# Inverted blocks loaded in 8 transfers instead of 16, diagonal blocks stored in 4 instead of 16, in a bidirectional gated-delta encoder layer

## The chip, the cores and the metric

The kernel runs on one core of a Trainium2 chip. The metric is the device time of one launch in microseconds (us). A core has five engines that run in parallel and wait for each other by semaphores: PE (TensorE, matrix products into PSUM), DVE (VectorE), ACT (ScalarE), POOL (GpSimd) and SP (SyncE), which here issues nearly all DMA transfers. Each engine works through its own instructions strictly in order, so an instruction that waits holds up everything behind it on that engine.

## The reference

One encoder layer over two sequences, a prompt of 1024 tokens and a sample of 256. A combined input projection feeds two groups of heads: four heads of a bidirectional gated DeltaNet and four heads of differential attention; then come an output projection, a layer norm, a SwiGLU and a second layer norm. The change lies in the delta rule, which is computed in chunks, forwards and backwards:

```python
def delta_rule_chunked(q, k, v, g, beta):
    ...
    gc = jnp.cumsum(g, axis=-1)
    decay = jnp.exp(jnp.where(incl, gc[..., :, None] - gc[..., None, :], -jnp.inf))
    kb = k * beta[..., None]
    m = jnp.where(strict, jnp.einsum('bhnid,bhnjd->bhnij', kb, k) * decay, 0.0)
    a_mat = m + jnp.eye(CHUNK, dtype=jnp.float32)
    rhs = jnp.concatenate([v * beta[..., None], kb * jnp.exp(gc)[..., None]], -1)
    sol = lax.linalg.triangular_solve(a_mat, rhs, left_side=True, lower=True, unit_diagonal=True)
    ...
    attn = jnp.einsum('bhnid,bhnjd->bhnij', q, k) * decay
    ...
    _, o = lax.scan(step, s0, xs)

    o_f = delta_rule_chunked(q, k, v, g[:, :, 0], beta[:, :, 0])
    o_b = flip(delta_rule_chunked(flip(q), flip(k), flip(v), flip(g[:, :, 1]), flip(beta[:, :, 1])))
```

The kernel uses chunks of 128 and inverts each chunk's unit triangular matrix explicitly.

## The kernel before

Four phases follow each other. Phase A (0 to about 523 us on PE) computes the input projection in columns of 128 (`dense_T`, matmuls of line 172) and, between these, prepares the DeltaNet. Phase B runs attention (score products of lines 835 and 836) together with the recurrent chains (`chain`, from line 1006 on). Phases C and D are the output projection, layer norms and the SwiGLU.

The preparation works in five *units*: units 1 to 4 are the heads of the prompt (8 chunks each), unit 5 is the sample (4 heads of 2 chunks). A unit passes through these steps:

- `prep_front` and, for two groups of four chunks, `prep_group`. Products of keys with keys and queries (`kq_ps`, line 418) are scaled by ACT into the tile KQ (line 424), the backward query products are copied there (line 426), and DVE multiplies by the decays `e_f`, `e_b`, `e_n` (lines 435 and 441). The results N[0] (forward) and N[1] (backward) are the matrices to be inverted; their diagonal blocks of 32 x 32 go to DRAM scratch `nblk` (line 438).
- `invert_blocks`: the blocks of the whole unit come back as 128 rows of 1024 in the tile Wb (line 465), each block in one partition, and DVE inverts them in Ub by products and sums (lines 470 and 471; tmp is the tile itmp). It begins with line 474.
- `spread_blocks`: Ub goes to DRAM scratch `ublk` with t = 0 (line 508), its transpose with t = 1, through Wb (lines 509 and 510), and from there onto the diagonals of four tiles UD (line 514).
- `invert_levels`: PE, ACT and DVE build the full inverses from the diagonal blocks, in four stages (`inv_ps`, line 535). The first stage multiplies N by the t = 1 tiles. The result goes to the records `rec` (line 578), from which phase B loads the chains' operands (`ld`, line 969).

UD, Wb, Ub and itmp exist once, so that a unit can fill them only when the unit before has been read out. The tiles of phase B lie in memory that phase A has used, so the first `ld` waits for the end of unit 5's inverse.

The order of the instructions on each engine is not written out in the source. The units are Python generators that `advance()` steps once per half of a dense product, levels first, then blocks, then fronts:

```python
        def advance():
            stage_of(levels, None)
            stage_of(blocks_, levels)
            stage_of(fronts, blocks_, HP_F)
            run_all(gens)
```

From what the source emits, the tile framework's scheduler then chooses each engine's order when the program is built, by priority and by when it reckons the operands to be ready. A small edit can thus move instructions far away from it.

Of the kernel before, what the change touches and what calls it, by code (L numbers as in the profile page):

```python
# [334 lines left out]
def prep_front(k, si, vh, c3, G, N, flag, room):  # L335
# [6 lines left out]
    for g in range(2):  # L342
# [12 lines left out]
        sq = gp.tile([P, 16, P], F32, tag="kq", name="sq")[:, 0:8]  # L355
# [15 lines left out]
    N.extend(k.gp2.tile([P, 8, P], F32, tag=f"N{d}", name=f"N{d}") for d in range(2))  # L371
    for g in range(2):
        yield from prep_group(k, si, vh, g, raw, G, N)


def prep_group(k, si, vh, g, raw, G, N):
# [36 lines left out]
    KQ = gp.tile([P, 4, 4, P], F32, tag="kq", name="KQ")  # L413
    for j in range(2):
# [11 lines left out]
        A.copy(KQ[:, 2 * j:2 * j + 2, 3], ps.rearrange("p (a b c) -> p a b c", a=2, b=2)[:, :, 1])  # L426
# [7 lines left out]
    def to_blocks(d, e):  # L434
        V.tensor_tensor(out=N[d][:, u0:u0 + 4, :], in0=KQ[:, :, 2 * d, :], in1=e, op=ALU.mult)
        for b in range(4):
            r = slice(32 * b, 32 * b + 32)
            nc.sync.dma_start(out=k.S.nblk[si][vh][d, u0:u0 + 4, b].rearrange("u r c -> r u c"), in_=N[d][r, u0:u0 + 4, r])

    def attn(d, e):  # L440
        V.tensor_tensor(out=e, in0=KQ[:, :, 1 + 2 * d, :], in1=e, op=ALU.mult)
# [16 lines left out]
def invert_blocks(k, si, vh):  # L458
# [42 lines left out]
    return Wb  # L501


def spread_blocks(k, si, vh, Wb):
# [4 lines left out]
    V.tensor_copy(Wb[0:64].rearrange("p (a b) -> p a b", a=32), U[0:64].rearrange("p (b a) -> p a b", a=32))  # L509
    nc.sync.dma_start(out=k.S.ublk[si][vh][1].rearrange("d u b r c -> (d u b) (r c)"), in_=Wb[0:64])  # L510
    for t in (1, 0):
        for b in range(4):
            for d in range(2):
                nc.sync.dma_start(out=diag(k, d, t, b), in_=k.S.ublk[si][vh][t][d, :, b].rearrange("u r c -> r u c"))


def diag(k, d, t, b):

# [4 lines left out]
def invert_levels(k, si, vh, N, G):
# [37 lines left out]
    for d in range(2):  # L561
        U, D = k.UD[d]
# [1097 lines left out]
```

## Time and profile before

| | before |
|---|---|
| time, median of 3 runs | 1794.15 us (1793.14 to 1796.1) |
| profiled execution: time, span | 1791.56 us, 1789.8 us |
| mean granted clock of PE | 0.970 |
| PE busy | 1710.3 us, 96% |
| DVE, ACT, POOL busy | 68%, 44%, 12% |
| PE idle, waiting for loads of UD | 12.1 us in 8 waits |
| PE idle, waiting for the first `ld` | 8.9 us in one wait |
| SP: loads of UD, stores to nblk | 80 and 80 |

Rows of instructions give start (us from the span's start), duration (us), engine, source line, operation, output tile <- input tiles, shape and count, and in brackets the idle time of the engine before them and what ended it. "SPq" is the issue of a DMA on SP: its duration is the time on the queue, not that of the transfer. In a table of windows each engine's busy time is followed by its number of instructions in brackets; the clock is the share of full speed that PE was granted.

### The profile page before, as it was taken

The page shows a single profiled execution, that of the slowest core. Times are in us where ns is not written, and L with a number is a line of the kernel's source. Part 1 is how long each engine was busy: PE and PEld are TensorE (multiplying, and loading weights), DVE is VectorE, ACT ScalarE, POOL GpSimd, SP SyncE. Part 2 cuts the span into 40 slices and gives each one's busy share as a digit, 9 for nine tenths or more (in the row PEclk, how much of TensorE's full clock was granted, in tenths as well). Part 3 has the DMA queues.
Part 4 walks back from the last instruction along what each step waited for, and adds up shares of the span by engine and source line. Part 5 has one row for each costly group of instructions (what it writes and reads, how often), then busy time and mean ns, then how long its engine had stood idle before and what let it go on. Part 6 is the DMA issues. An engine that isn't in the chain of part 4 may idle for free.

```text
span 1789.8 us, 27447 instructions
## 1 busy us (share of the span) xinstructions
PE 1710.3 (96%) x10234; PEld 1483.0 (83%) x10234; DVE 1214.0 (68%) x2092; ACT 783.7 (44%) x1538; POOL 218.5 (12%) x201
## 2 busy tenths in 40 slices
PE   8999989999986899999999999999999999999998
PEld 8988868888864898788888888888888887888886
DVE  4245888986694468977665866665666665666696
ACT  4146766664433767877113332322222223553330
POOL 2000000000022435732321000000000000000011
PEclk9999999998985999999999999999999999999999
DMA  7124456656754977634631534333344432975541
GB/s 237 40 57 115 126 131 168 168 168 182 190 154 103 297 238 220 177 118 156 188 119 51 193 112 140 120 121 133 124 145 146 146 113 100 386 272 177 174 159 71
DMA packets 254116, 279.05 MB, mean 156 GB/s; under 512 B 49297, under 2 KB 198687, under 8 KB 252575
## 3 DMA queue, kind: packets, MB, share of 16 engines
q1 hardware_dynamic: 244079, 265.20, 47.6%
q10 hardware_dynamic: 9904, 12.10, 2.0%
q8 instruction: 80, 1.31, 0.3%
q14 instruction: 53, 0.43, 0.1%
HBM read 183.80 MB, written 93.43 MB: 155 GB/s over the span
## 4 chain that ended last, share of the span: by engine, by line
PE 54%; ACT 1%; DVE 1%; issue 1%; DMA 0%; POOLq 0%; POOL 0%; DVEq 0%; SPq 0%; ACTq 0%
PE dn_ps L1503 14%; PE gy_ps L1277 9%; PE gs_ps L1277 7%; PE om_ps L172 6%; PE gx_ps L1277 6%; PE gz_ps L1277 6%; PE gp_ps L1277 2%; PE o_ps L875 1%; PE x_ps L1182 0%; ACT ap L839 0%; PE s_ps L835 0%; PE tt_ps L862 0%; PE s_ps L836 0%; DVE ast L837 0%; ACT woh L1162 0%
## 5 line engine op out<-in xcount | busy, mean ns | idle before, releaser
L1293 ACT CAST sph<-wraw 128x512 fp32r<-128x512 f32 x92 | 57.0, 623 | 195.7 <-PE gy_ps L1277 124.5
L310 POOL TENSOR_TENSOR rs_r<-lva,mhalf 128x1 f32<-128x1 f32 x20 | 29.5, 1475 | 837.4 <-DVE lva L1139 818.9
L172 PE MATMUL dps<-xh,wlo 128*128 128x512 f32 (+1 forms) x552 | 122.7, 363 | 2.0 <-DVE wlo L163 2.0
L172 PE MATMUL dps<-xl,whi 128*128 128x512 f32 (+1 forms) x552 | 122.4, 364 | 0.0
L172 PE MATMUL dps<-xh,whi 128*128 128x512 f32 (+1 forms) x552 | 122.2, 362 | 0.0
L1293 ACT CAST sph<-wsum 128x512 fp32r<-128x512 f32 x80 | 49.7, 622 | 156.6 <-PE gy_ps L1277 61.9
L1503 PE MATMUL dn_ps<-tth,ssh 128*128 128x512 f32 x280 | 108.9, 389 | 0.0
L1503 PE MATMUL dn_ps<-ttl,ssh 128*128 128x512 f32 x280 | 108.8, 389 | 0.0
L172 PEld LDWEIGHTS dps<-xh,wlo 128*128 128x128 f32 x552 | 94.4, 193 | 17.3 <-DVE wlo L163 2.4
L1503 PE MATMUL dn_ps<-tth,ssl 128*128 128x512 f32 x280 | 108.1, 389 | 0.0
L172 PEld LDWEIGHTS dps<-xl,whi 128*128 128x128 f32 x552 | 94.8, 195 | 15.8 <-ACT whi L162 0.4
L172 PEld LDWEIGHTS dps<-xh,whi 128*128 128x128 f32 x552 | 94.1, 193 | 14.4
L329 DVE SCALAR_TENSOR_TENSOR c<-pad,cw,c 128x1024 f32<-128x1024 f32 (+1 forms) x96 | 81.7, 876 | 28.8 <-ACT c L327 28.3
L837 DVE TENSOR_REDUCE ast<-s_ps 128x1 f32<-128x1024 f32 (+1 forms) x80 | 83.5, 1055 | 22.6 <-PE s_ps L836 20.4
L1294 DVE TENSOR_TENSOR spl<-wraw,sph 128x512 fp32r<-128x512 f32 x92 | 63.0, 686 | 47.9 <-PE gs_ps L1277 29.6
L839 ACT ACTIVATE ap<-s_ps,ast 128x1024 f32<-128x1024 f32 (+1 forms) x80 | 79.8, 1000 | 34.7 <-DVE ast L837 32.1
L1294 DVE TENSOR_TENSOR spl<-wsum,sph 128x512 fp32r<-128x512 f32 x80 | 55.0, 688 | 46.8 <-issue 20.4
L835 PE MATMUL s_ps<-akl,aq 128*128 128x512 f32 (+1 forms) x144 | 65.8, 458 | 20.3 <-ACT ap L839 19.0
L1494 ACT CAST ssh<-sraw 128x640 fp32r<-128x640 f32 x77 | 55.9, 727 | 48.5 <-PE dn_ps L1503 34.3
L1495 DVE TENSOR_TENSOR ssl<-sraw,ssh 128x640 fp32r<-128x640 f32 x77 | 62.9, 820 | 16.8 <-ACT ssh L1494 13.4
L851 POOL TENSOR_TENSOR ap<-ap,ap 128x512 f32<-128x512 f32 (+2 forms) x60 | 62.4, 1059 | 81.2 <-ACT ap L848 49.5
L875 PE MATMUL o_ps<-av,tt 128*128 128x128 f32 x544 | 66.2, 280 | 0.0
(391 smaller groups left out, 4307.6 us busy)
## 6 DMA issues: line engine op xcount, KB each, us to landing
ld<-rec SPq DMA_DIRECT2D x160, 192.0 KB, 3.9
sraw<-hs SPq DMA_DIRECT2D x77, 320.0 KB, 4.7
wraw<-in_w_gate_up_dram SPq DMA_DIRECT2D x22, 1024.0 KB, 5.2
wraw<-in_w_in_dram SPq DMA_DIRECT2D x24, 512.0 KB, 4.2
wdraw<-in_w_down_dram SPq DMA_DIRECT2D x11, 1024.0 KB, 4.9
ws<-wdraw SPq DMA_DIRECT2D x11, 1024.0 KB, 3.9
traw<-ws SPq DMA_DIRECT2D x44, 256.0 KB, 4.1
araw<-dqk SPq DMA_DIRECT2D x40, 256.0 KB, 5.0
```

What stands on the lines that cost most here:

```text
L172: nc.tensor.matmul(out, lhsT=a(i), rhs=b(i), start=start and j == 0, stop=stop and j == len(seq) - 1)
L329: V.scalar_tensor_tensor(out=out, in0=pad[:, so + w:so + w + n], scalar=k.cw[:, w * 12 + ti:w * 12 + ti + 1], in1=out, op0=ALU.mult, op1=A ...
L835: nc.tensor.matmul(ps[:, o:o + w], lhsT=a.q[m][:, qs], rhs=a.kl[m][:, k0 + o:k0 + o + w], start=True, stop=False)
L837: V.tensor_reduce(out=st[:, m:m + 1], in_=ps, op=ALU.max, axis=AX.X, negate=True)
L839: A.activation(p, ps, AF.Exp, bias=st[:, m:m + 1], accum_out=a.s0[:, i:i + 1] if m == 0 else st[:, 2:3])
L851: nc.gpsimd.tensor_tensor(out=pr[0][:, c], in0=pr[0][:, c], in1=pr[1][:, c], op=ALU.add)
L875: nc.tensor.matmul(ps[:, j * P:(j + 1) * P], lhsT=tt[:, i, j * P:(j + 1) * P], rhs=a.v[:, v0 + i, :], start=i == 0, stop=i == NT[a.si] - 1)
L1277: m = nc.tensor.matmul(ps, lhsT=a(i), rhs=b(i), start=start and j == 0, stop=stop and j == len(seq) - 1, skip_group_check=again)
L1293: A.copy(hi, src)
L1294: V.tensor_tensor(out=lo, in0=src, in1=f32(hi), op=ALU.subtract)
L1495: V.tensor_tensor(out=lo, in0=src, in1=f32(hi), op=ALU.subtract)
L1503: nc.tensor.matmul(ps, lhsT=a[:, c], rhs=b, start=z == 0 and j == 0, stop=z == NPR - 1 and j == 2)
```

## The change

The four UD tiles (two of them half as wide) become two of 128 x 16 x 128, one for t = 0 and one for t = 1, with the forward and the backward direction beside each other, and N[0] and N[1] become halves of one tile of the same shape. One transfer now moves a block row of both directions: 8 loads of twice the size for 16 of `ublk`, and 4 stores for 16 of `nblk`, which are issued once both groups are ready. The transposed blocks leave through itmp instead of Wb. The backward query products are no longer copied into KQ: DVE multiplies them by `e_b` from PSUM, half a group at a time, and `e_b` is therefore computed before the products.

```diff
@@ prep_front
-    N.extend(k.gp2.tile([P, 8, P], F32, tag=f"N{d}", name=f"N{d}") for d in range(2))
+    both = k.gp2.tile([P, 16, P], F32, tag="N", name="N")
+    N.extend(both[:, 8 * d:8 * d + 8] for d in range(2))
     for g in range(2):
         yield from prep_group(k, si, vh, g, raw, G, N)
+    for b in range(4):
+        r = slice(32 * b, 32 * b + 32)
+        nc.sync.dma_start(out=k.S.nblk[si][vh][:, :, b].rearrange("d u r c -> r (d u) c"), in_=both[r, :, r])
@@ prep_group
-    KQ = gp.tile([P, 4, 4, P], F32, tag="kq", name="KQ")
+    e_b = gp.tile([P, 4, P], F32, tag="e_b", name="e_b")
+    masked(e_b, e_n, k.lower, ALU.add)
+    decay(e_b, 1, 1.0)
+    KQ = gp.tile([P, 4, 3, P], F32, tag="kq", name="KQ")
...
-        A.copy(KQ[:, 2 * j:2 * j + 2, 3], ps.rearrange("p (a b c) -> p a b c", a=2, b=2)[:, :, 1])
+        V.tensor_tensor(out=e_b[:, 2 * j:2 * j + 2], in0=ps.rearrange("p (a b c) -> p a b c", a=2, b=2)[:, :, 1],
+                        in1=e_b[:, 2 * j:2 * j + 2], op=ALU.mult)
+    nc.sync.dma_start(out=rec[:, :, 7, :], in_=e_b)
...
     def to_blocks(d, e):
         V.tensor_tensor(out=N[d][:, u0:u0 + 4, :], in0=KQ[:, :, 2 * d, :], in1=e, op=ALU.mult)
-        for b in range(4):
-            r = slice(32 * b, 32 * b + 32)
-            nc.sync.dma_start(out=k.S.nblk[si][vh][d, u0:u0 + 4, b].rearrange("u r c -> r u c"), in_=N[d][r, u0:u0 + 4, r])
-
-    def attn(d, e):
-        V.tensor_tensor(out=e, in0=KQ[:, :, 1 + 2 * d, :], in1=e, op=ALU.mult)
-        nc.sync.dma_start(out=rec[:, :, 1 + 6 * d, :], in_=e)
@@ spread_blocks
-    V.tensor_copy(Wb[0:64].rearrange("p (a b) -> p a b", a=32), U[0:64].rearrange("p (b a) -> p a b", a=32))
-    nc.sync.dma_start(out=k.S.ublk[si][vh][1].rearrange("d u b r c -> (d u b) (r c)"), in_=Wb[0:64])
+    V.tensor_copy(k.itmp[0:64].rearrange("p (a b) -> p a b", a=32), U[0:64].rearrange("p (b a) -> p a b", a=32))
+    nc.sync.dma_start(out=k.S.ublk[si][vh][1].rearrange("d u b r c -> (d u b) (r c)"), in_=k.itmp[0:64])
     for t in (1, 0):
         for b in range(4):
-            for d in range(2):
-                nc.sync.dma_start(out=diag(k, d, t, b), in_=k.S.ublk[si][vh][t][d, :, b].rearrange("u r c -> r u c"))
+            nc.sync.dma_start(out=diag(k, t, b), in_=k.S.ublk[si][vh][t][:, :, b].rearrange("d u r c -> r (d u) c"))
@@ phase_a
-        k.UD = [[per.tile([P, 8, P if d == t else 64], F32, name=f"UD{d}{t}") for t in range(2)] for d in range(2)]
+        k.UD = [per.tile([P, 16, P], F32, name=f"UD{t}") for t in range(2)]
```

`invert_levels` has the same products as before, with other slices of the tiles. In the rows below, the numbers behind tile names only tell tiles apart; before, UD_1060 to UD_1063 are the four tiles (1061 and 1063 are t = 1), in the changed kernel UD_1060 is t = 0 and UD_1061 is t = 1.

SP, between the inversions of units 3 and 4. Before, the end of unit 3's sixteen loads of UD, then the last store of unit 4's blocks (nblk_68) and the load of its Wb:

```order
L514 DMA UD_1060<-ublk_70 32x8x32
L514 DMA UD_1062<-ublk_70 32x8x32
L514 DMA UD_1060<-ublk_70 32x8x32
L514 DMA UD_1062<-ublk_70 32x8x32
L514 DMA UD_1060<-ublk_70 32x8x32
L514 DMA UD_1062<-ublk_70 32x8x32
L438 DMA nblk_68<-N_3452 32x4x32
L354 DMA rec_65<-vn 512x1x128
L465 DMA Wb<-nblk_68 64x1024 x2
```

The same place in the changed kernel:

```order
L377 DMA nblk_68<-N 32x16x32 x4
L182 DMA wraw<-in_w_in_dram 128x8x128
L445 DMA rec_66<-e_f 512x1x128
L464 DMA Wb<-nblk_68 64x1024
L506 DMA ublk_70<-Ub 64x1024
L464 DMA Wb<-nblk_68 64x1024
L508 DMA ublk_70<-itmp 64x1024
L399 DMA e_f<-gc_57 128x512
L354 DMA rec_65<-vn 512x1x128
L511 DMA UD_1060<-ublk_70 32x16x32 x4
L511 DMA UD_1061<-ublk_70 32x16x32 x4
```

The loads of unit 4's Wb moved from behind unit 3's spread to before it, behind a load of weights (wraw), and the t = 1 tile is now loaded after the t = 0 tile.

PE, after the last dense product. Before, fourteen pairs of score products (s_ps) stand ahead of unit 5's first inverse products (inv_ps from N); the last of them and these:

```order
L835 MATMUL s_ps<-akl,aq 128x512
L836 MATMUL s_ps<-akh,aq 128x512
L535 MATMUL inv_ps<-UD_1061,N_4209 32x32 x8
L535 MATMUL inv_ps<-UD_1063,N_4210 32x32 x8
L835 MATMUL s_ps<-akl,aq 128x512
L836 MATMUL s_ps<-akh,aq 128x512
L835 MATMUL s_ps<-akl,aq 128x512
L836 MATMUL s_ps<-akh,aq 128x512
L535 MATMUL inv_ps<-UD_1061,N_4209 32x32 x8
L535 MATMUL inv_ps<-UD_1063,N_4210 32x32 x8
```

In the changed kernel, from the last dense product on:

```order
L172 MATMUL dps<-xh_291,whl 128x256 x16
L828 MATMUL s_ps<-akl,aq 128x512
L829 MATMUL s_ps<-akh,aq 128x512
L828 MATMUL s_ps<-akl,aq 128x512
L829 MATMUL s_ps<-akh,aq 128x512
L828 MATMUL s_ps<-akl,aq 128x512
L530 MATMUL inv_ps<-UD_1061,N 32x32 x32
L829 MATMUL s_ps<-akh,aq 128x512
L828 MATMUL s_ps<-akl,aq 128x512
L829 MATMUL s_ps<-akh,aq 128x512
```

The first inverse products of unit 5 moved from behind 28 score matmuls to behind five. Four score matmuls make a group (one map of one tile of queries).

DVE, the end of unit 5's inversion. Before, up to the transpose into Wb, with score maxima (ast) and a query part (aq) between its products:

```order
L470 TENSOR_TENSOR itmp<-Ub,iT 128x1024
L837 TENSOR_REDUCE ast<-s_ps 128x1
L471 TENSOR_REDUCE Ub<-itmp 128x8x8
L837 TENSOR_REDUCE ast<-s_ps 128x1
L470 TENSOR_TENSOR itmp<-Ub,iT 128x1024
L837 TENSOR_REDUCE ast<-s_ps 128x1
L802 SCALAR_TENSOR_TENSOR aq<-araw,aq 64x1024
L471 TENSOR_REDUCE Ub<-itmp 128x8x8
L841 RECIPROCAL ast<-ast 128x1
L837 TENSOR_REDUCE ast<-s_ps 128x1
L507 COPY Ub<-Ub 64x16x8
```

In the changed kernel:

```order
L469 TENSOR_TENSOR itmp<-Ub,iT 128x1024
L470 TENSOR_REDUCE Ub<-itmp 128x8x8
L795 SCALAR_TENSOR_TENSOR aq<-araw,aq 64x1024
L469 TENSOR_TENSOR itmp<-Ub,iT 128x1024
L470 TENSOR_REDUCE Ub<-itmp 128x8x8
L505 COPY Ub<-Ub 64x16x8
L507 COPY itmp<-Ub 64x1024
L830 TENSOR_REDUCE ast<-s_ps 128x1
L539 COPY Z<-inv_ps 32x16x32 x2
```

All four score maxima moved behind the inversion.

More of the change, by code (lines that the diff above doesn't have):

```diff
@@ L354, in prep_front @@
                 nc.sync.dma_start(out=k.S.rec[si][vh][g][:, :, 5, :], in_=vn)
-        sq = gp.tile([P, 16, P], F32, tag="kq", name="sq")[:, 0:8]
+        sq = gp.tile([P, 12, P], F32, tag="kq", name="sq")[:, 0:8]
         for role in range(2):
@@ L435, in to_blocks @@
         V.tensor_tensor(out=N[d][:, u0:u0 + 4, :], in0=KQ[:, :, 2 * d, :], in1=e, op=ALU.mult)
-        for b in range(4):
-            r = slice(32 * b, 32 * b + 32)
-            nc.sync.dma_start(out=k.S.nblk[si][vh][d, u0:u0 + 4, b].rearrange("u r c -> r u c"), in_=N[d][r, u0:u0 + 4, r])
-    def attn(d, e):
-        V.tensor_tensor(out=e, in0=KQ[:, :, 1 + 2 * d, :], in1=e, op=ALU.mult)
-        nc.sync.dma_start(out=rec[:, :, 1 + 6 * d, :], in_=e)
     to_blocks(0, e_f)
-    attn(0, e_f)
+    V.tensor_tensor(out=e_f, in0=KQ[:, :, 1, :], in1=e_f, op=ALU.mult)
+    nc.sync.dma_start(out=rec[:, :, 1, :], in_=e_f)
     yield
-    attn(1, e_b)
     to_blocks(1, e_n)
@@ L500, in invert_blocks, with spread_blocks @@
         prod(8, 8, 16, (U, a * 32, [[32, 8], [0, 8], [1, 16]]), (T, 0, [[0, 8], [1, 8], [8, 16]]), (U, 16 + a * 32, [[32, 8], [1, 8]]))
-    return Wb
-def spread_blocks(k, si, vh, Wb):
+def spread_blocks(k, si, vh):
     nc, V, U = k.nc, k.nc.vector, k.Ub
@@ L526, in invert_levels @@
     q = [slice(32 * b, 32 * b + 32) for b in range(4)]
-    hq = [slice(32 * (b % 2), 32 * (b % 2) + 32) for b in range(4)]
-    uq, dq = (q, hq), (hq, q)
     lo, up = slice(0, 64), slice(64, 128)
-    ub = (up, lo)
+    UD = [[t[:, 8 * d:8 * d + 8] for t in k.UD] for d in range(2)]
     def pe(ps, rows, c0, m, fn):
@@ L619, in phase_a @@
             nc.gpsimd.memset(pad, 0.0)
-        k.UD = [[per.tile([P, 8, P if d == t else 64], F32, name=f"UD{d}{t}") for t in range(2)] for d in range(2)]
-        for row in k.UD:
-            for t in row:
-                nc.gpsimd.memset(t, 0.0)
+        k.UD = [per.tile([P, 16, P], F32, name=f"UD{t}") for t in range(2)]
+        for t in k.UD:
+            nc.gpsimd.memset(t, 0.0)
         k.upper, k.lower = [per.tile([P, P], F32, name=n) for n in ("m_up", "m_low")]
@@ L668, in invert @@
             def invert():
-                flag.Wb = yield from invert_blocks(k, si, vh)
+                yield from invert_blocks(k, si, vh)
             def back():
-                spread_blocks(k, si, vh, flag.Wb)
+                spread_blocks(k, si, vh)
                 yield from invert_levels(k, si, vh, N, k.G[si])
```

32 lines of the change are left out of this document (14 added, 18 removed).

## The prediction

> **What bounds the kernel now.** I read the page's shares first, then what TensorE (PE) waits for, and then the stretch in which those waits lie. The page's first part, and its rows of PE's busy tenths and of the granted clock in 40 slices of 44.7 us:
>
> ```profile
> PE 1710.3 (96%) x10234; PEld 1483.0 (83%) x10234; DVE 1214.0 (68%) x2092; ACT 783.7 (44%) x1538; POOL 218.5 (12%) x201
> ...
> PE   8999989999986899999999999999999999999998
> ...
> PEclk9999999998985999999999999999999999999999
> ```
>
> PE is busy for 96% of the span, and the change adds and removes no matmul. What it can move is PE's idle time and the time at a low clock, and both gather in the slices from about 525 to 590 us. Two of the three longest waits of PE (in total, times, longest one, us):
>
> ```profile
> PE inv_ps L535 <- DMA UD<-ublk: 12.1, 8, 5.0
> PE vn_ps L1023 <- DMA ld<-rec: 8.9, 1, 8.9
> ```
>
> Both belong to the code that is changed: the blocks of the inverse that are loaded into UD, and the records from which the recurrent chains start. PE in order of time, from the first score group (s_ps), which follows the last dense product, to the first chain product (vn_ps):
>
> ```profile
> 523.15 0.40 PE L835 MATMUL s_ps<-akl,aq 128*128 128x512 f32 x1
> ...
> 547.60 1.93 PE L535 MATMUL inv_ps<-UD,N 32*32 32x32 f32 x32 [1.10 <-DMA UD<-ublk]
> 549.46 0.80 PE L835 MATMUL s_ps<-akl,aq 128*128 128x512 f32 x1
> ...
> 551.46 1.91 PE L535 MATMUL inv_ps<-UD,N 32*32 32x32 f32 x32
> ...
> 583.57 0.77 PE L1023 MATMUL vn_ps<-ld,ld 128*128 128x128 f32 x2 [8.94 <-DMA ld<-rec]
> ```
>
> The dense products end at 523.2 us. The inverse of the last unit (unit 5, the sample) gets its operands only at 547.6, and the chains, which need the memory that the inverse frees, start at 583.57. This tail of 60 us holds eleven score groups and one inverse, about 18 us of work at full clock (eleven groups of 1.0, half of the 2.0 from 549.46 to 551.46 at half clock; 224 matmuls of the inverse, of which the two rows above show 64 in 3.84 at half clock). I take it as what the change acts on. Windows around it (duration, busy PE, PEld, DVE, ACT, POOL, then clock, DMA share, GB/s):
>
> ```profile
> 400.00:425.00 25.00, 22.73 (x235) 19.62 (x234) 10.38 (x18) 7.74 (x16) 2.89 (x1) 0.82 0.67 167
> 425.00:472.00 47.00, 47.00 (x287) 40.15 (x286) 44.96 (x76) 33.23 (x80) 0.00 (x0) 0.99 0.70 202
> 472.00:492.00 20.00, 18.65 (x220) 15.44 (x219) 4.53 (x9) 1.57 (x4) 0.00 (x0) 1.00 0.67 169
> 492.00:541.00 49.00, 37.59 (x213) 30.66 (x212) 46.09 (x71) 18.49 (x28) 9.64 (x3) 0.80 0.59 153
> ...
> 550.00:560.00 10.00, 10.00 (x114) 7.90 (x113) 6.69 (x8) 3.08 (x4) 2.27 (x2) 0.50 0.15 24
> ```
>
> Here VectorE (DVE) sets the pace: it is full in 425-472 and 492-541, where it inverts the diagonal blocks of units 4 and 5, and it stands idle for 14.6 and 15.5 us in the two stretches between. Why it stands idle is in the rows of DVE and of SP, the queue that issues the loads:
>
> ```profile
> 403.60 1.35 SPq L438 DMA_DIRECT2D nblk<-N  x1
> 405.06 9.86 SPq L514 DMA_DIRECT2D UD<-ublk  x16
> 414.96 0.45 SPq L438 DMA_DIRECT2D nblk<-N  x1
> ...
> 417.32 1.14 SPq L465 DMA_DIRECT2D Wb<-nblk  x2
> ...
> 421.99 0.18 DVE L474 COPY Ub<-Wb 128x16 f32<-128x16 f32 x1 [4.49 <-issue]
> ...
> 464.89 0.67 DVE L435 TENSOR_TENSOR N<-KQ,e_n 128x512 f32<-128x512 f32 x1
> ...
> 475.80 10.22 SPq L514 DMA_DIRECT2D UD<-ublk  x16
> 486.07 1.14 SPq L465 DMA_DIRECT2D Wb<-nblk  x2
> 492.17 0.18 DVE L474 COPY Ub<-Wb 128x16 f32<-128x16 f32 x1 [7.86 <-issue]
> ...
> 539.93 1.03 DVE L509 COPY Wb<-Ub 64x1024 f32<-64x1024 f32 x1
> ...
> 544.85 8.94 SPq L514 DMA_DIRECT2D UD<-ublk  x16
> ```
>
> A unit's inversion begins with L474 and ends with L509. Each load of Wb stands on SP behind sixteen UD loads of the unit before (9.86 and 10.22 us), because Wb also carries the transposed blocks out (L510) until their store has landed. So unit 4 begins at 421.99 though all of its stores but one had left SP by 405, and unit 5 at 492.17 though its last N was ready at 465.6.
>
> **The change part by part.**
>
> *The DMAs.* Durations on SP (first number after the count: shortest, median, longest issue in ns), and the window 544-556 us, in which the sixteen UD loads run nearly alone:
>
> ```profile
> L514 SPq DMA_DIRECT2D UD<-ublk x80: 303/449/1673, 261.5 to 553.3; - x80
> L578 SPq DMA_DIRECT2D rec<-UD x20: 512/634/802, 309.8 to 578.5; - x20
> ...
> q1 hardware_dynamic: 4442, 0.78, 32.7%
> ...
> UD<-ublk SPq DMA_DIRECT2D x16, 32.0 KB, 1.9
> ```
>
> Sixteen loads take 8.94 to 10.22 us on SP, 0.56 to 0.64 each in a run, while the DMA engines are 33% busy: the issue sets the pace. A load of twice the packets is not in the trace; its bounds are 0.56 (an issue costs the same) and 1.12 (it costs by packets). The nearest row is L578, 512 packets at 0.63; I take that, so eight loads take 5.0. The sixteen stores become four at the same price, 2.5 us where they took about 7, but none leaves before both groups are done.
>
> The Trainium skill (DMA: Bandwidth & Descriptors, section Bandwidth) calls transfers under 64 KB descriptor-dominated, and the descriptors do not become fewer here. By it eight loads would take the 8.9 us of sixteen, and the sum below would be 2 us smaller. With the engines 33% busy, this trace does not agree.
>
> *Wb no longer carries the blocks out* (itmp does), so its load needs only the four stores. On SP the loads of unit 4 move ahead of unit 3's spread. Its N were stored around 400 to 404; four stores (2.5), 2.5 to land, two Wb issues (1.14) and 4.4 to land give a start at about 412 instead of 421.99. That fills 10 of the 14.6 idle us, so that DVE has unit 4 and the N of unit 5 done at 463 rather than 472.8. From there on SP: the eight UD loads of unit 4 wait until unit 3's UD has been stored (463 + 1.3 + 3.4), their last four take 2.5 more, the stores 2.5 + 2.5, Wb 1.1 + 4.4: unit 5 starts at 480 or 481, 12 earlier, and DVE stands idle for some 10 us before it instead of 15.5.
>
> *What lies within unit 5's inversion.* Before, four score maxima and three aq were queued between its products. Over 150-580 us by form, and over 400-542 us:
>
> ```profile
> L837 DVE TENSOR_REDUCE ast<-s_ps 128x1 f32<-128x1024 f32 x11 | 13.3, 1218 | 5.2 <-PE s_ps L836 5.0
> ...
> L802 DVE SCALAR_TENSOR_TENSOR aq<-araw,aq 64x1024 fp32r<-64x1024 f32 x3 | 5.4, 1807 | 1.3 <-ACT aq L801 1.3
> ...
> L763 DVE TENSOR_TENSOR rx<-rx,rcs 128x256 f32<-128x256 f32 x5 | 2.1, 418 | 0.1
> ```
>
> Now no maximum and two aq are: 4 x 1.22 + 1.8 = 6.7 us less, and six more rope products, 2.5 more. 48.8 us (492.17 to 540.96) become 44.6 by this, so it would end at 525. By DVE's work instead (106 us of work in 400-541, less 6.7, with some 20 idle) it ends at 519. I take 522, 19 earlier.
>
> *From there to the first matmul.* The first UD load follows 3.9 us later (540.96 to 544.85), now at 526. PE's first operand was the third load and arrived 2.75 later; now it is the fourth of eight (three t = 0 loads go ahead): 3 x 0.63 + 1.9 = 3.8 plus its own issue, at 530. The halved number thus gains nothing here, its order takes it back. The dense products and the five score matmuls that stand ahead end at 524.4, so data decide: 530 instead of 547.6, **17.6 earlier**.
>
> *From the first matmul to vn_ps.* Before: 36.0 us with four score groups in it. Now 7.75 groups stand there. One takes 2.0 at the clock of this stretch: 7.5 more, from 0 to 7.5 of it hidden under the 8.94 of waiting for records and the waits for Z. I take the middle: **3.7 later**. Two groups come after vn_ps instead of before it, where the clock is full, at 1.0 each: **2.0 later**. From there the order on PE is that of before, group by group, so a shift here is a shift of the end.
>
> *Small operations*, ahead of the tail:
>
> ```profile
> L426 ACT COPY KQ<-kq_ps x20: 372/410/452, 163.3 to 450.6; 128x256 f32<-128x256 f32 x20
> ...
> L441 DVE TENSOR_TENSOR e_b<-KQ,e_b x10: 671/683/693, 167.1 to 461.6; 128x512 f32<-128x512 f32 x10
> ...
> L559 DVE COPY UD<-inv_ps x15: 417/418/432, 284.2 to 565.6; 32x256 f32<-32x256 f32 x15
> ```
>
> ScalarE (ACT) loses 20 copies, 8.2 us, at 44% busy: nothing. DVE reads PSUM in two halves, at 0.42 each by L559 (L763 gives the same from SBUF): 20 x 0.42 - 10 x 0.68 = 1.6 us more over ten groups, some 0.6 of it after 400, within the rounding above. The PSUM tile kq_ps is now held until DVE, not ACT, has read it. The next group's matmuls come about 12 us later; the cover is that distance, and if DVE falls behind by more, PE stands at kq_ps.
>
> *The dense stretch.* PE waited 12.1 us for UD there and in the tail. The first blocks of units 2 and 4 now stand 60 and 81 matmuls earlier, those of units 1 and 3 about where they stood. A gain of all of it or a like loss are the bounds; I take zero, since a later dense end is hidden until it passes 530.
>
> **Sum:** -17.6 + 3.7 + 2.0 = -11.9, and two stores that now follow the first eight record loads instead of standing among them give 1.3: **-13 us**. The profiled execution took 1791.56 (span 1789.8), 2.6 under the median of 1794.15; on the median this is **1781**.
>
> **The rivals.**
> *1. The clock stays up.* In 550-560 PE was busy for 10.0 of 10 us and the clock stood at 0.50, so the trace says that this work does not bring it back; but with PE going from dense products to inverse with a wait of 6 us instead of idling on and off from 525, it may not drop. PE's work from first matmul to vn_ps is then some 14 us instead of 29: the 3.7 vanish and half of the inverse's 13 us too: 1771. The Trainium skill (TensorE: Matmul & The Clock Gate, Part 1: The HAM clock gate) has the full clock return after one busy window of about 3.4 us, which would make this the likely case; the row of 550-560 contradicts it.
>
> *2. Unit 5 does not start earlier.* Both loads of Wb now stand behind a weight load (wraw), which waits for DVE:
>
> ```profile
> SPq L182 <- DVE wlo L163: 53.1, 11, 14.6
> ```
>
> If such a wait (longest 14.6) eats the 12 us, only the 6.7 of deferred work is left, less the 4.4 of the later terms: 1792, no change to measure or a little faster.
>
> *3. Slower: PE stands before UD in the dense stretch.* Unit 1 shows the price in the trace:
>
> ```profile
> 268.69 1.91 PE L535 MATMUL inv_ps<-UD,N 32*32 32x32 f32 x32 [5.01 <-DMA UD<-ublk]
> ...
> 272.00:276.00 4.00, 4.00 (x26) 3.29 (x25) 3.93 (x6) 1.06 (x1) 0.11 (x1) 0.51 0.90 197
> 276.00:280.00 4.00, 4.00 (x22) 3.40 (x21) 3.41 (x12) 3.02 (x6) 0.00 (x0) 1.00 0.92 270
> ```
>
> A wait of 5.0 is followed by some 7.3 us at half clock, 3.7 lost: 8.7 in all. For unit 4 the earlier place and the wait for unit 3's store leave 6 or 7 us open, 10 with the clock. It decides when the dense end passes 542: then the first matmul is not 4.4 earlier than before, which is what the later terms cost. With units 2, 3 and 4 each losing 10, the dense end is 553, the first matmul 554, and the time 1794 + 6.5 + 4.4 = 1805. Against it: so far PE's place and the data met within 2.3 us for units 2 to 4.
>
> **How the numbers follow.** The sum's case (start of the chains 6 to 20 us earlier, 1774 to 1788) gets 0.60, the clock 0.13, rival 2 0.13 (of which 0.08 within 0.2%), rival 3 0.14 (of which 0.01 within). Faster by over 0.2% (3.6 us, about what can be told from no change): 0.60 + 0.13 + 0.05 = 0.78; same 0.09; slower 0.13. The range reaches from rival 1 to a little beyond rival 2, 1766 to 1797, and leaves most of rival 3 out.
>
> **What would show it.** Right: L464 (Wb) of units 4 and 5 at about 406 and 475 on SP, the first inv_ps of unit 5 at 526 to 534, vn_ps near 570, UD loads of 0.6 us each, DVE less idle in 400-425. Wrong: UD loads of 1.1 us; a wait for UD of over 5 us in the dense stretch; dense products that end after 535; a wait at kq_ps; or a gain that lies after the chains have started.

## The result, and the profile after

| | before | after |
|---|---|---|
| median of the runs on one chip | 1793.64 us | 1768.35 us |
| ratio, 95% interval | | 0.9864 (0.9842 to 0.9886) |
| profiled execution: time, span | 1791.56, 1789.8 us | 1766.4, 1764.5 us |
| mean granted clock of PE | 0.970 | 0.975 |

The change makes the kernel 1.4% faster. The forecast was 1781, 13 us below the 1794.15 of before; the medians differ by 25.3 us, and so do the two profiled spans. The direction and the place were right, the size was half. One run of a kernel of the next section (e9, 2834 us at a clock of 0.56) is left out of its ratio.

From the first page of the changed kernel's profile come the busy times of the engines, PE's busy tenths and its granted clock, in slices of 44.1 us; from its view of waits, three of PE's (in total, times, longest one), and below them one of before:

```profile
PE 1707.8 (97%) x10234; PEld 1480.5 (84%) x10234; DVE 1218.7 (69%) x2102; ACT 776.5 (44%) x1518; POOL 221.8 (13%) x199
...
PE   8999999999998999999999999999999999999998
...
PEclk9999999999895999999999999999999999999999
...
PE inv_ps L530 <- DMA UD<-ublk: 13.2, 6, 4.4
PE s_ps L828 <- ACT ap L832: 7.6, 9, 1.7
PE vn_ps L1016 <- issue: 4.1, 1, 4.1
```
```profile
PE s_ps L835 <- ACT ap L839: 19.0, 15, 4.0
```

The dent in PE's busy row is down from 8, 6, 8 to one 8; the slice with the clock at 5 is still there. PE waits for UD about as long as before in all (13.2 and 12.1 us), but elsewhere: in the dense stretch 8.8 us instead of 11.0, its longest wait 3.3 instead of 5.0, and in the tail 4.4 instead of 1.1. The wait that fell most is the one for ACT's exponentials, from 19.0 us to 7.6; before, 9.4 of it lay between 523 and 548, where score groups were all that PE had to do until unit 5's blocks came. Two of the windows of the prediction, now for the changed kernel:

```profile
400.00:425.00 25.00, 23.50 (x250) 20.39 (x249) 19.32 (x46) 10.24 (x27) 2.90 (x1) 0.86 0.68 190
...
472.00:492.00 20.00, 20.00 (x175) 16.28 (x175) 17.50 (x52) 4.62 (x10) 0.00 (x0) 0.91 0.42 124
```

In 400-425 DVE is busy for 19.3 us instead of 10.4, and in 472-492 for 17.5 instead of 4.5: units 4 and 5 are inverted in what used to be idle time. The lead begins at unit 2. The end of unit 1's inversion and the start of unit 2's, on SP and DVE, first before, then after:

```profile
256.41 0.49 SPq L508 DMA_DIRECT2D ublk<-Ub  x1
...
263.93 0.48 SPq L510 DMA_DIRECT2D ublk<-Wb  x1
264.45 6.75 SPq L514 DMA_DIRECT2D UD<-ublk  x11
271.25 1.11 SPq L465 DMA_DIRECT2D Wb<-nblk  x2
277.56 0.18 DVE L474 COPY Ub<-Wb 128x16 f32<-128x16 f32 x1
```
```profile
251.24 1.14 SPq L464 DMA_DIRECT2D Wb<-nblk  x2
256.44 0.47 SPq L506 DMA_DIRECT2D ublk<-Ub  x1
...
259.74 4.58 SPq L511 DMA_DIRECT2D UD<-ublk  x8
259.91 0.19 DVE L473 COPY Ub<-Wb 128x16 f32<-128x16 f32 x1
```

Before, unit 2's load of Wb is the last of a run that starts with unit 1's results, and stands behind the store that reads Wb (L510). After, it is issued 5.2 us ahead of these results, because Wb no longer carries them, and unit 2 starts 17.7 us earlier. Units 3, 4 and 5 keep this lead: 22, 19 and 19 us. The last two in the changed kernel, and unit 5's way to the chains:

```profile
391.85 1.93 SPq L377 DMA_DIRECT2D nblk<-N  x4
395.52 0.50 SPq L464 DMA_DIRECT2D Wb<-nblk  x1
...
401.19 5.03 SPq L511 DMA_DIRECT2D UD<-ublk  x8
402.74 0.18 DVE L473 COPY Ub<-Wb 128x16 f32<-128x16 f32 x1 [1.26 <-DMA Wb<-nblk]
...
453.23 0.68 DVE L441 TENSOR_TENSOR N<-KQ,e_f 128x512 f32<-128x512 f32 x1
...
461.09 2.10 SPq L377 DMA_DIRECT2D nblk<-N  x4
...
465.46 1.12 SPq L464 DMA_DIRECT2D Wb<-nblk  x2
473.23 0.18 DVE L473 COPY Ub<-Wb 128x16 f32<-128x16 f32 x1
...
517.39 1.11 DVE L507 COPY itmp<-Ub 64x1024 f32<-64x1024 f32 x1
517.86 2.06 PE L172 MATMUL dps<-xh,whl 128*128 128x256 f32 x16
520.32 4.41 SPq L511 DMA_DIRECT2D UD<-ublk  x8
525.44 3.40 PE L530 MATMUL inv_ps<-UD,N 32*32 32x32 f32 x64 [4.36 <-DMA UD<-ublk]
560.22 0.76 PE L1016 MATMUL vn_ps<-ld,ld 128*128 128x128 f32 x2 [4.10 <-issue]
```

Unit 5 starts at 473.2 (492.2 before) and ends at 518.5 (541.0); its first inverse product comes at 525.4 (547.6) and the first chain product at 560.2 (583.6). 23.3 of the 25.3 us are thus there when the chains start. In the next 35 us 3.3 more are gained, and 1.3 are lost after them. Attention's value products (o_ps) that follow, before, then after:

```profile
595.11 3.74 PE L875 MATMUL o_ps<-av,tt 128*128 128x128 f32 x32
...
609.17 0.50 PE L835 MATMUL s_ps<-akl,aq 128*128 128x512 f32 x1 [4.03 <-ACT ap L839]
...
618.54 3.74 PE L875 MATMUL o_ps<-av,tt 128*128 128x128 f32 x32
```
```profile
573.35 3.73 PE L868 MATMUL o_ps<-av,tt 128*128 128x128 f32 x32
...
591.91 3.74 PE L868 MATMUL o_ps<-av,tt 128*128 128x128 f32 x32
```

From the chains' start to the first of these rows it is 11.5 us before and 13.1 after, from the first to the second 23.4 and 18.6: the wait of 4.03 us for ACT's exponentials at 609 is gone from this stretch. A wait of the same kind, of 1.72 us, stands behind it now, at 603. Why the wait became shorter was not tested.

### The profile page after: what moved, and what is told of

It is laid out like the page before. It is cut to its first block, busy times and chain, and to the rows that moved or that the text cites. A ratio compares the mean times of both kernels' runs of the same rounds, so it can differ in the third digit from the quotient of the medians.

```text
span 1764.5 us, 27348 instructions
## 1 busy us (share of the span) xinstructions
PE 1707.8 (97%) x10234; PEld 1480.5 (84%) x10234; DVE 1218.7 (69%) x2102; ACT 776.5 (44%) x1518; POOL 221.8 (13%) x199
## 4 chain that ended last, share of the span: by engine, by line
PE 54%; ACT 1%; DMA 1%; DVE 1%; issue 1%; POOLq 0%; POOL 0%; DVEq 0%; SPq 0%; ACTq 0%
PE dn_ps L1496 15%; PE gy_ps L1270 9%; PE gs_ps L1270 7%; PE gx_ps L1270 6%; PE gz_ps L1270 6%; PE om_ps L172 6%; PE gp_ps L1270 2%; DMA worw<-in_w_out_dram 1%; PE o_ps L868 1%; PE x_ps L1175 0%; ACT ap L832 0%; PE s_ps L828 0%; PE s_ps L829 0%; ACT woh L1155 0%; DMA sraw<-hs 0%
## 5 line engine op out<-in xcount | busy, mean ns | idle before, releaser
L172 PE MATMUL dps<-xh,whi 128*128 128x512 f32 (+1 forms) x552 | 130.4, 371 | 0.0
L172 PE MATMUL dps<-xl,whi 128*128 128x512 f32 (+1 forms) x552 | 126.2, 368 | 0.0
```

What stands on the lines that cost most here:

```text
L172: nc.tensor.matmul(out, lhsT=a(i), rhs=b(i), start=start and j == 0, stop=stop and j == len(seq) - 1)
```

## The experiments

All kernels were timed against the kernel before on the same chip; line numbers in rows are those of each kernel's own source. The table gives for each the rows on which the readings rest: start of units 2 and 5 on DVE, end of unit 5's transposed copy, first inverse product of unit 5, first vn_ps, span (all of the profiled execution, in us), and the ratio of the times with its interval. "Left" says which of the three transfer edits (itmp instead of Wb, 8 loads, 4 stores) a kernel has, and whether it has the wide tiles and the products out of PSUM (t+P).

| kernel | left | unit 2 | unit 5 | end | inverse | vn_ps | span | ratio |
|---|---|---|---|---|---|---|---|---|
| before | none | 277.6 | 492.2 | 541.0 | 547.6 | 583.6 | 1789.8 | 1 |
| e9 | P | 276.5 | 486.2 | 540.1 | 546.7 | 582.1 | 1790.9 | 0.9980 (0.9967 to 0.9994) |
| e1 | itmp | 263.7 | 490.1 | 537.5 | 544.3 | 582.1 | 1789.9 | 0.9995 (0.9982 to 1.0008) |
| e5 | t+P | 277.2 | 483.5 | 532.2 | 539.4 | 573.6 | 1784.7 | 0.9959 (0.9946 to 0.9971) |
| e7 | t+P, stores | 272.8 | 489.1 | 539.1 | 545.7 | 581.7 | 1787.7 | 0.9984 (0.9972 to 0.9996) |
| e6 | t+P, loads | 272.7 | 478.1 | 522.3 | 529.1 | 563.9 | 1771.5 | 0.9893 (0.9880 to 0.9907) |
| e3 | t+P, itmp, stores | 260.7 | 478.0 | 528.6 | 535.1 | 569.7 | 1775.7 | 0.9906 (0.9891 to 0.9921) |
| e2 | t+P, loads, stores | 269.5 | 482.3 | 526.0 | 531.8 | 570.0 | 1774.9 | 0.9875 (0.9852 to 0.9897) |
| e4 | t+P, itmp, loads | 263.8 | 479.2 | 525.2 | 532.5 | 564.1 | 1768.3 | 0.9885 (0.9867 to 0.9902) |
| after | all | 259.9 | 473.2 | 518.5 | 525.4 | 560.2 | 1764.5 | 0.9864 (0.9842 to 0.9886) |
| e8 | all, t = 0 loads on ACT | 262.1 | 477.6 | 525.0 | 533.1 | 561.1 | 1769.6 | 0.9883 (0.9864 to 0.9902) |
| e10 | all, unit 5 on ACT | 260.4 | 471.0 | 521.4 | 527.8 | 563.1 | 1769.3 | 0.9885 (0.9868 to 0.9902) |
| e11 | all, unit 5 on POOL | 260.2 | 476.9 | 524.1 | 530.6 | 564.8 | 1773.2 | 0.9877 (0.9859 to 0.9895) |
| e12 | all, Wb twice | 260.5 | 483.3 | 528.6 | 534.7 | 569.7 | 1776.4 | 0.9888 (0.9871 to 0.9905) |

First reading of the table: span less vn_ps is 1204 to 1211 in all fourteen kernels, while vn_ps moves by 23 us. The time is set by when the chains start. And from the end of unit 5's blocks to its first inverse product it is 5.8 to 8.1 us, with 8 loads as with 16 (6.9 after, 6.5 in e3, 6.6 before).

**e1. itmp alone, in the kernel before.**

```diff
-    V.tensor_copy(Wb[0:64].rearrange("p (a b) -> p a b", a=32), U[0:64].rearrange("p (b a) -> p a b", a=32))
+    V.tensor_copy(k.itmp[0:64].rearrange("p (a b) -> p a b", a=32), U[0:64].rearrange("p (b a) -> p a b", a=32))
```

> The kernel before, with one edit: the transposed blocks leave through itmp instead of Wb; 16 loads and 16 stores as before. Theory: freeing Wb is needed but does not act alone. In the program's order the loads of Wb of units 4 and 5 still stand behind the sixteen UD loads, and the last stores of unit 5's blocks stand behind them too, so units 4 and 5 start within 4 us of before (422 and 492), and the time is within 5 us of before (1789 to 1799). Rival (freeing Wb is the whole gain): both units start 10 us or more earlier and the time falls by 10 to 25 us.

Measured 0.9995: no difference, as the theory had it. Unit 2 does start 14 us earlier, but units 4 and 5 do not (421.4, 490.1). SP shows why, here at the end of unit 4; at that of unit 3 it is alike:

```profile
472.52 7.71 SPq L514 DMA_DIRECT2D UD<-ublk  x14
480.28 3.19 SPq L438 DMA_DIRECT2D nblk<-N  x4
485.15 1.30 SPq L465 DMA_DIRECT2D Wb<-nblk  x2
```

Wb is free, but the last stores of the unit's blocks fall into the same moment as the sixteen loads, and Wb's load, which needs those stores, comes behind both.

**e2. The changed kernel, through Wb again.** The edit of e1 in reverse.

> The changed kernel, with one edit undone: the transposed blocks leave through Wb again; 8 loads and 4 stores stay. Theory: unit 4's load of Wb stands behind the spread of unit 3 again, so unit 4 starts at 408 to 413 (402.7 in the changed kernel, 422 before), and unit 5 some 5 us later than the 473 of the changed kernel; time 1771 to 1778. Rival (fewer DMAs on SP are the gain, the tile does not matter): unit 5 starts within 2 us of 473 and the time is that of the changed kernel, 1768.

Measured 0.9875. Unit 2 starts 9.5 us later than after and unit 5 9.1 later, more than expected, yet the time is only some 4 us longer at the median (1772.7), and the intervals overlap. The rival on unit 5's start is refuted; that the tile decides the time is not shown either.

**e3. Sixteen loads again.**

```diff
-            nc.sync.dma_start(out=diag(k, t, b), in_=k.S.ublk[si][vh][t][:, :, b].rearrange("d u r c -> r (d u) c"))
+            for d in range(2):
+                nc.sync.dma_start(out=diag(k, t, b, d), in_=k.S.ublk[si][vh][t][d, :, b].rearrange("u r c -> r u c"))
```

> The changed kernel with each UD load split by direction, 16 loads of 8 KB per unit again instead of 8; everything else stays. Theory: the halved number gains only its issue time. SP spends 4.5 us more per unit on UD loads; in unit 5 the first operand is then the sixth load instead of the fourth (1 us later) and the second stage's about 4 us later, so the first inverse product of unit 5 is at 526 to 529 (525.4) and the time 1768 to 1773. Rival (the halved loads are the gain): 1780 or more.

Measured 0.9906 (1776.9): between the two. (A split load has 32 KB, not 8.) Where the theory failed is ahead of the tail: unit 5 starts 4.8 us later, and its inversion takes 50.6 us instead of 45.3. Of the 5.3 us more, DVE's waits for rope tables and rope data account for 3.9 (5.5 instead of 1.6) and one product of UD, which ran beside one of POOL's, for 2.2 (3.4 instead of 1.2). The dense products end later too, at 530.0 instead of 519.9, but PE still waits 3.25 us for UD behind them. The tail itself is no longer: 6.5 us from the last block to the first product.

**e4. Sixteen stores again.**

```diff
         V.tensor_tensor(out=N[d][:, u0:u0 + 4, :], in0=KQ[:, :, 2 * d, :], in1=e, op=ALU.mult)
+        for b in range(4):
+            r = slice(32 * b, 32 * b + 32)
+            nc.sync.dma_start(out=k.S.nblk[si][vh][d, u0:u0 + 4, b].rearrange("u r c -> r u c"), in_=N[d][r, u0:u0 + 4, r])
```

> The changed kernel with 16 stores of diagonal blocks per unit again instead of 4, issued as each N of a group is ready; everything else stays. Theory: in the program's order unit 4's load of Wb stands behind the UD loads of unit 3 again, because its last stores do, so that unit 4 starts at 410 or later (402.7) and unit 5 at 478 or later (473.2); time 1774 to 1785. Rival (the stores are hidden work on a queue that has time): unit 4 and 5 start as in the changed kernel, time 1768.

The starts came out as expected (unit 4 at 417.7, unit 5 at 479.2), the time did not: 0.9885, 1771.6. Unit 5's six us are partly given back between its first inverse product and vn_ps, which take 31.7 us instead of 34.8; the clock is back at 0.89 there from 551 us to the start of the chains, where it stood at 0.50 in the changed kernel.

None of the three edits, undone alone, costs more than some 0.4%, so they may stand in for each other. The next three take all of them away, or all but one.

**e5. None of the three transfer edits.** The edits of e2, e3 and e4 together.

> The changed kernel with all three edits of the transfers undone: 16 loads, 16 stores, transposed blocks through Wb. The wide tiles and the query products out of PSUM stay. Theory: the three edits shorten what SP does between the end of one unit's blocks and the next unit's load of Wb, each takes some of the same wait, and any two of them take nearly all of it; with none, units 4 and 5 start as before (within 4 us of 422 and 492) and the time is 1787 to 1795. Rival (the products out of PSUM, or the new order of the instructions that comes with them, carry the gain): unit 5 starts at 484 or earlier and the time is 1780 or less.

**e6. The 8 loads alone of the three.** The edits of e2 and e4.

> The changed kernel with 16 stores and with the transposed blocks through Wb, so that of the transfers only the 8 loads remain changed. Theory (each edit takes part of the same wait): unit 5 starts some 5 us earlier than with none of them, at 483 to 488; time 1776 to 1787. Rival (one edit alone does nothing, as the first run with itmp alone): within 3 us of the run with none of the three.

**e7. The 4 stores alone of the three.** The edits of e2 and e3.

> The changed kernel with 16 loads and with the transposed blocks through Wb, so that of the transfers only the 4 stores remain changed. In the program's order six score maxima and three aq stand in unit 5's inversion, as before the change, and 28 score products ahead of its inverse. Theory: unit 5 starts 3 to 5 us earlier than with none of the three, its inversion lasts 47 to 49 us; time 1780 to 1791. Rival (the deferred score maxima are what counts): as with none of the three, 1787 to 1795, though unit 5 starts earlier.

Measured: 0.9959, 0.9893 and 0.9984 (1786.4, 1774.7 and 1791.4 us). e5 lies between its theory and its rival: unit 5 starts 8.6 us earlier than before, but the time falls by 7.4; e6 beats its theory. The 8 loads alone bring 0.7% on top of the 0.4% of the tiles and PSUM, half of the whole change; itmp and the 4 stores without them (e3) bring 0.5%; all three 1.0%. The 4 stores alone bring nothing: e7 is even 0.25% slower than e5. The tiles alone were not run. What the loads do shows most plainly on SP ahead of unit 2, in e5 and in e6:

```profile
263.04 9.35 SPq L513 DMA_DIRECT2D UD<-ublk  x15
272.43 1.11 SPq L464 DMA_DIRECT2D Wb<-nblk  x2
```
```profile
263.01 4.90 SPq L512 DMA_DIRECT2D UD<-ublk  x7
267.96 1.14 SPq L464 DMA_DIRECT2D Wb<-nblk  x2
```

The load of Wb follows unit 1's loads directly in both; these take 4.5 us less, and unit 2 starts 4.6 us earlier. Ahead of unit 5 it is less simple. Unit 4's loads take 4.3 us instead of 10.2, but in e6 four stores come behind them and Wb waits for these, so that from the first load to Wb it is 11.3 us, and 10.3 in e5. What unit 5 gains, 5.4 us at its start, it gains because unit 4 starts 3.2 us and ends 9.4 us earlier. Its own inversion is shorter as well, 44.1 us instead of 48.7, of which DVE's waits for rope tables and rope data, which SP loads behind Wb, account for 3 us and one score maximum for 1.2. In e7 the score maxima are back in the inversion (four; the six of the text count two other small operations on ast), unit 5 starts and ends within some 3 us of before, and on the time the rival fits better than the theory, though unit 5 does not start earlier than in e5, as both had it, but 5.6 us later.

**e8. The t = 0 loads on ACT.**

```diff
-            nc.sync.dma_start(out=diag(k, t, b), in_=k.S.ublk[si][vh][t][:, :, b].rearrange("d u r c -> r (d u) c"))
+            (nc.sync if t else nc.scalar).dma_start(out=diag(k, t, b), in_=k.S.ublk[si][vh][t][:, :, b].rearrange("d u r c -> r (d u) c"))
```

> The changed kernel with the four loads of the t = 0 blocks issued by ACT instead of SP, so that the t = 1 blocks, which the first stage reads, no longer stand behind three of them. Theory: the first inverse product of unit 5 comes 1.7 us (3 x 0.55) sooner after the end of its transposed copy, 5.2 instead of 6.9; the chains start 1 to 2 us earlier; time 1764 to 1768. Rival (ACT, which waits for the stored blocks, holds up what stands behind it): 1770 to 1775.

Measured 0.9883 (1771.3): not faster. The first product comes 8.1 us after the last block, not 5.2. SP's four loads, now the t = 1 blocks alone:

```profile
528.86 2.10 SPq L511 DMA_DIRECT2D UD<-ublk  x4
...
533.07 3.40 PE L530 MATMUL inv_ps<-UD,N 32*32 32x32 f32 x64 [5.17 <-DMA UD<-ublk]
```

They start 3.9 us after the copy ended: their blocks were stored at 525.15, and such a store lands in 3.6 us (median). In the changed kernel the store is at 518.5 with 3.5 to land, so the needed load could not go before 522.0, and it goes at 520.3 + 3 x 0.55 = 522.0. The three loads ahead of it fill that wait and cost nothing.

**e9. The products out of PSUM alone, in the kernel before.** KQ 3 wide, `e_b` ahead of the products and multiplied from `kq_ps`, as in the change; everything else as before.

> The kernel before, with one edit: the backward query products are multiplied out of PSUM by DVE, half a group at a time, and KQ is 3 wide. Four narrow UD tiles, 16 loads, 16 stores and Wb as before. Theory: this part and not the wide tiles gave the 0.4% of the run with the three transfer edits undone, because it shortens what stands before a group's N; unit 5 starts at 483 to 488 and the time is 1784 to 1790. Rival (ACT's and DVE's few us are hidden, as forecast, and the rest is a chance of the order): 1791 to 1797.

Measured 0.9980: 3.6 us at the medians. Unit 5 starts 6 us earlier, as the theory had it, but four score maxima and 18 rope products lie in its inversion, which takes 54 us, and vn_ps is 1.5 us earlier. By the medians it gives half of the 0.4% of e5, though the two intervals just overlap; the time lies between theory and rival.

**e10 and e11. Unit 5's stores and its loads of Wb on ACT, and on POOL.** With `nc.scalar` (e10) or `nc.gpsimd` (e11) in place of `q` for unit 5:

```diff
-        nc.sync.dma_start(out=k.S.nblk[si][vh][:, :, b].rearrange("d u r c -> r (d u) c"), in_=both[r, :, r])
+        (q if not si else nc.sync).dma_start(out=k.S.nblk[si][vh][:, :, b].rearrange("d u r c -> r (d u) c"), in_=both[r, :, r])
...
-        nc.sync.dma_start(out=Wb[64 * j:64 * j + 64], in_=nb)
+        (q if not si else nc.sync).dma_start(out=Wb[64 * j:64 * j + 64], in_=nb)
```

> The changed kernel with unit 5's four stores of diagonal blocks and its two loads of Wb issued by ACT instead of SP; all engines' orders are those of the changed kernel up to unit 5's blocks. Theory: unit 5 no longer waits for unit 4's eight UD loads on SP and starts at 463 to 468 instead of 473.2; the first inverse product of unit 5 comes 3 to 8 us sooner and the time is 1758 to 1765. Rival (unit 5's start no longer sets the end, since the dense products end at 519.9 and 24 rope products now lie in its inversion): the start is as early, but the time stays at 1766 to 1770, or is worse where ACT waits for the stored blocks and PE for ACT.

> As the run with unit 5's stores and loads on ACT, but issued by POOL, which has nothing else to do there. Theory: unit 5 starts at 463 to 470 and the time is 1758 to 1765. Rival (POOL's issue or the landing of its transfers is slower than SP's, or unit 5's start no longer sets the end): 1766 to 1775.

Neither is faster than the changed kernel (0.9885 and 0.9877). In e10 the unit starts 2 us earlier, not 5 to 10: the stores, free of SP, still take their time beside unit 4's loads.

```profile
454.77 6.20 ACTq L377 DMA_DIRECT2D nblk<-N  x4
463.51 1.54 ACTq L464 DMA_DIRECT2D Wb<-nblk  x2
```

Its inversion is longer, with six more rope products and a copy that took three times its 1.1 us (last section). In e11 the loads of Wb leave POOL by 465.6, 1 us earlier than in the changed kernel on SP, and the unit starts 3.7 us later. Two things hold it there. Unit 4, which lies ahead of the edit, already starts at 406.5 instead of 402.7. And the loads of Wb have landed by 471, but DVE comes to L473 only behind rope products, whose data SP loads, and two splits of weights (L163, the second at 475.77):

```profile
474.54 1.23 DVE L163 TENSOR_TENSOR whl<-wraw,whl 128x1024 fp32r<-128x1024 f32 x1 [0.17 <-ACT whl L162]
...
476.91 0.18 DVE L473 COPY Ub<-Wb 128x16 f32<-128x16 f32 x1
```

In the changed kernel such a split is also the last row ahead of L473, and ends within half a microsecond of the landing of Wb: in that order an earlier load alone could not have gained much.

**e12. Unit 5's Wb loaded twice**, `range(2 if si else 4)` for `range(2)`, so that the unit starts later and does the same work.

> The changed kernel with unit 5's Wb loaded twice, the second time over the first, so that the inversion starts some 5 us later; nothing else of the work changes. Theory (unit 5's start sets the start of the chains, us for us): start at 477 to 480, vn_ps 4 to 6 us later (564 to 566), time 1770 to 1775. Rival (up to 5 us are slack, hidden by the dense products or by score groups): vn_ps within 2 us of 560, time 1766 to 1770.

The second pair waits for the first, which delays the start by 10.0 us, more than meant; the end of the inversion is 10.1 later, the first inverse product 9.3, vn_ps 9.4 and the span 11.9:

```profile
483.26 0.18 DVE L473 COPY Ub<-Wb 128x16 f32<-128x16 f32 x1 [2.88 <-DMA Wb<-nblk]
```

By the traces the start passes on us for us, and the rival (vn_ps within 2 us of 560) is out. Some 3 of the 10 us do not stem from the second pair, as unit 4 already starts at 405.8 instead of 402.7; differences of this size between two single traces say little. By the ratios the loss is 4 us of 10, with intervals that overlap; the execution traced for e12 took 1778.2 us at a median of 1774.7, that of the changed kernel 1766.4 at 1768.4. None of the kernels tried has a lower ratio than the changed one.

## Why the prediction was right, and where its sizes were wrong

| step | forecast | measured |
|---|---|---|
| unit 4 starts | 412 | 402.7 |
| unit 5 starts | 480 to 481 | 473.2 |
| its inversion | 44.6 by its parts, 41 to 42 by the end taken | 45.3 |
| its end | 522 | 518.5 |
| first UD load after it | 3.9 | 1.8 |
| last block to first inverse product | 8 | 6.9 |
| first inverse product, against before | -17.6 | -22.2 |
| from there to vn_ps | +3.7 | -1.2 |
| the chains' first 13 us | +2.0 | +1.6 |
| the next 19 us | 0 | -4.9 |
| the rest (the forecast: stores behind record loads) | -1.3 | +1.3 |
| sum | -13 | -25.3 |

**The place** was right: the chains' start sets the time (span less vn_ps, all kernels), and in the traces unit 5's start sets that (e12). PE's wait for UD in the dense stretch, taken to stay, fell by 2.2 us. The price of a load was right: 0.55 us for one of 64 KB (4.41 for eight), at the low bound of 0.56 to 1.12. By the rule of the Trainium skill that the prediction weighed (DMA: Bandwidth & Descriptors, section Bandwidth) they would, as the prediction worked it out, have taken 8.9; the trace disagrees. (The page's sentence is on transfers under 64 KB, and the new loads have just 64.)

**Inside the range by a little, and partly by luck.** The sum's own case was 1774 to 1788. The measured 1768 lies below it, 2 us above the low end of the range, and that end was set for a clock that stays up, which did not come. Of the signs named, loads of 0.6 us, no wait for UD of over 5 us and a dense end before 535 came true; the loads of Wb came at 395.5 and 465.5 instead of 406 and 475, and vn_ps at 560 instead of 570.

**Where the other 12 us are.** 4.6 of them had come by the first inverse product, 4.9 between it and the chains, 5.3 in the next 32 us, and the rest took 2.6 back.

**The first step that was too small** is the start of unit 4, forecast 9.3 us too late. The sum began at unit 4 and took its N as ready when they were before, around 400. In fact the same edit acts on every unit from the second on: unit 2 gained 17.7 us, and unit 4's blocks were stored at 391.9. In every kernel of the table with itmp unit 2 starts at 260 to 264, in every one with Wb at 269 to 278. The rows for it stood in the trace of before; the sum rests on the stretch from 400 on alone. Unit 5's N was thus ready 9.1 us earlier than forecast (453.9); its way from there to the start was given 1.8 us too little (17.5, with 19.3 measured). Of the 9.3 us, 7 to 8 are left at unit 5's start and 3.5 at its end, because the inversion had been taken some 4 us too short.

**The weight of the parts** was wrong as well. The forecast gave the earlier starts to the freed tile and let the halved loads gain little. In the tail this is right (6.5 to 6.9 us with 16 and with 8), though not for the reason given: the three loads ahead of the needed one run while it waits for its own blocks (e8). Ahead of a load of Wb, however, 8 loads are worth 4.5 us of SP (unit 2, e5 and e6), and alone they bring 0.7%, where itmp alone, in the kernel before, brings nothing (e1). The tile lets the next unit's load pass; the fewer loads and stores make what stands in between short. The loads alone (e6), or itmp with the stores (e3), get half or more of what all three bring, and these gains do not add up.

**The score groups cost nothing.** +3.7 was the middle of 0 to 7.5; the low end was right. From first inverse product to vn_ps it took 34.8 us with 7.75 groups and 36.0 with four, and 34 to 38 in ten of the twelve other kernels, with 4 to 8.5 groups. This fits a stretch that the inverse's own steps through PE, ACT and DVE set, with the groups in PE's waits.

**The wait at 609** (4.0 us, then some 3.5 us at half clock) stood in the trace of before, and the forecast took nothing for it.

**The rivals.** Slower, by PE standing before UD: the waits in the dense stretch stayed at 3.3 us or less. Unit 5 no earlier, by wraw: its load took 0.6 us on SP there, though the split of these weights on DVE stands ahead of L473 (e11). The clock that stays up: it fell as before, and the windows of the tail, with e8 beneath, show that it need not:

```profile
525.44:560.22 34.78, 29.83 (x255) 23.42 (x256) 22.24 (x28) 21.13 (x31) 12.33 (x8) 0.50 0.42 104
...
541.00:560.00 19.00, 15.11 (x80) 11.31 (x80) 11.98 (x17) 11.35 (x17) 8.46 (x6) 0.50 0.25 75
```
```profile
541.00:560.00 19.00, 14.20 (x129) 10.60 (x127) 13.91 (x21) 15.21 (x24) 9.92 (x7) 0.86 0.47 112
```

e8 took 28.0 us from first inverse product to vn_ps instead of 34.8, e4 31.7. What brings the clock back in one and not in the other was not found. PE was busy for 29.8 of 34.8 us in the changed kernel's stretch, and the clock stayed at 0.50: the rule of the Trainium skill that the prediction weighed (TensorE: Matmul & The Clock Gate, Part 1: The HAM clock gate), full clock after one busy window, is again not what the trace shows, as far as a row's busy time tells.

## What to carry to other kernels

A tile that is both the input of one step and the output buffer of the next serializes the two through the queue that fills it; look where it is written, and look at the first place where it repeats, not only at the last. The gain of an earlier start can pass on through all later units, so sum it from the first: here 17.7 us at unit 2 were still 19 at unit 5, while in e1 14 us were lost again behind the loads of unit 3. Where several edits shorten one wait, take them away one by one and all together: undone alone each looked here like 0.1 to 0.4%, together they are 1.0%.

## What the runs showed of the hardware that was not expected

**Twice the size at the same issue price, but a later landing.** A UD load of 32 KB took 1.9 us from issue to landing (median over the run before), one of 64 KB 2.9 (after), while the issue on SP stayed at 0.56 (8.94 for sixteen) and 0.55 us (4.41 for eight). From the view of DMA issues, before and after, whole run:

```profile
UD<-ublk SPq DMA_DIRECT2D x80, 32.0 KB, 1.9
```
```profile
UD<-ublk SPq DMA_DIRECT2D x40, 64.0 KB, 2.9
```

By these medians a microsecond of what the fewer issues save is given back where a load is waited for.

**DVE copies stand while POOL works.** In e10 unit 5's transposed copy took 3.16 us (1.02 to 1.14 in the other kernels), while POOL worked on a product. Below it, in the changed kernel, the copy ahead of it took 1.82 us (0.22 in e10 and before):

```profile
517.95 2.46 POOL L163 TENSOR_TENSOR akl<-araw,akh 128x1024 fp32r<-128x1024 f32 x1 [9.19 <-ACT akh L162]
...
518.20 3.16 DVE L507 COPY itmp<-Ub 64x1024 f32<-64x1024 f32 x1
```
```profile
514.87 2.40 POOL L163 TENSOR_TENSOR akl<-araw,akh 128x1024 fp32r<-128x1024 f32 x1 [7.38 <-ACT akh L162]
515.54 1.82 DVE L505 COPY Ub<-Ub 64x128 f32<-64x128 f32 x1
```

In e10 POOL is done at 520.4 and the copy 0.95 us later, in the changed kernel at 517.3 and 0.1 later: as if the copies had begun only then. The Trainium skill (SBUF — State Buffer, section SBUF: two separate sides) has it that VectorE, in a 2-port mode or with two inputs from SBUF against a GpSimd operation that reads SBUF, and GpSimd hold a shared pair of ports exclusively, for a whole instruction. The rows agree. An operation of POOL that falls on the last copies of a critical chain costs up to its length: 2.1 us in e10, and 1.6 in the changed kernel itself.
